# First layer of a two-layer trunk: x's projection by two plain pairs and ten of Strassen's seven products, memory gates moved into the output projection

## The chip, the cores and the metric

The kernel runs on one core of one Trainium2 chip. The metric is the device time of that core in microseconds (us). A core has five engines that run their own instruction streams and wait for each other by semaphores: TensorE (PE; its weight load PEld is listed apart), VectorE (DVE), ScalarE (ACT), GpSimd (POOL) and SyncE (SP), which here issues the DMAs between DRAM and SBUF. Products are accumulated in PSUM banks.

## The reference

Two layers act on x (1024 tokens by 1024 features), with 256 memory tokens beside it. The first layer, cut to what matters:

```python
h = x @ w_in                                    # columns: main 1024 | memory queries 512 | main gates 1024 | memory gates 512
u, q, g_main, g_mem = split(h)
y_main = pool(u)                                # group i of 256 features: mean over the last 2/4/8/16 tokens, less the token,
                                                # times pool_w[i] (256 x 256) and pool_scale
y_mem = softmax(q k^T / sqrt(128)) v            # 4 heads; k | v = mem @ w_mem_kv
y = concat(y_main * silu(g_main), y_mem * silu(g_mem))
x = layer_norm(alpha * x + y @ w_out)
```

The second layer has the same frame; its main branch is an attention with 16 heads. Everything is float32.

## The kernel before, in words

**Arithmetic.** TensorE's fast format keeps fewer bits than float32. So each operand is split: `high` is the operand rounded to that format, `low` the rest (`hi_lo`, lines 134 to 137: ScalarE copies, VectorE subtracts; `split_w`, from line 139, does it with a tile of weights that a DMA brings into the ring `raw` of three tiles). A product is then three matmuls: high x high, high x low, low x high.

**Layout.** x is held transposed, features on the 128 partitions, as eight tiles high and eight low (`A`). 128 output features by 1024 tokens are a *slab* (`slab`, L168): two accumulators of 128x512 in the PSUM ring `pj` (three banks), 8 feature tiles x 2 halves x 3 = 48 matmuls of 128x512, two weight tiles of 128 x 512. What comes out is handed to a function: copied (`u`), split (queries), or made a gate (`gate`: tanh on ScalarE, one operation on VectorE). Other PSUM rings are `L` (two banks), `T` (two, for transposes) and `O` (one).

**Order of the first layer.** 24 slabs are computed from x. `load_x` brings the eight tiles of x and splits them, while the first slabs' matmuls follow. `pool_group(0)`: two slabs of u, window sums on VectorE (1 to 4 additions of 128x1024 for each half, then `pm`, mean less token, and its split), two slabs of gates, the small product with `pool_w` (24 matmuls), times the gates, store to `y0d` in DRAM. Then `mem_kv` (keys and values of the memory), `mem_attention` (four slabs of queries; then, for eight blocks of 128 tokens, logits, softmax, transposes of the probabilities, `values`; between these steps `Fill` pumps the four slabs of memory gates so that TensorE has something to do; at its end the gates are multiplied in and the four heads stored), and `pool_group(1)` to `(3)`. GpSimd takes no part in any of this.

**Output projection** (`out_proj`, L315). 24 weight tiles of 128x512 go through `raw`, are split, and stay in tiles that later stages do not need yet. For four strips of 256 tokens the three quarters of y (`src`, in the order 2, 0, 1, where 2 is the memory's) are loaded from DRAM, split and multiplied: 144 matmuls a strip. Then comes the layer norm and the transposes that make the next layer's x.

**Who sets the order.** The program is written in this sequence; a scheduler of the language decides each engine's order from it by its own model of costs, except where `manual_schedule` fixes the written order, before for TensorE inside `mem_attention` alone. SyncE issues its DMAs in order, and an instruction that waits holds back those behind it on its engine.

Of the kernel before, what the change touches and what calls it, by code (L numbers as in the profile page):

```python
# [23 lines left out]
MH = 4  # L24
# [43 lines left out]
def trunk_kernel(ctx, tc, x, xT, memT, win, wk, wv0, wv, wmk, wmv, wout, poolw, pscale, lng, lnb, bforget, out):  # L68
# [28 lines left out]
    def ps(shape, tag, bufs):  # L97
        return psum.tile(shape, F32, tag=tag, name=nm(tag), bufs=bufs)
# [7 lines left out]
    def MK(shape, dt=F32R):  # L106
        return sb(list(shape), "MK", 4, dt)
# [10 lines left out]
    def w_slots(tags, where):  # L118

        def tiles(k):  # L120
            tag, bufs = tags[k]
            if tag == "w":
                return [[wt([P, NH]) for _ in range(2)] for _ in range(2)]
            if tag == "MK":
                pair = [MK([P, 2, NH]) for _ in range(2)]
            elif tag == "PG":
                pair = [sb([P, 2, NH], "P", 4, F32R), sb([P, 2, NH], "G", 4, F32R)]
            else:
                pair = [sb([P, 2, NH], tag, bufs, F32R, where) for _ in range(2)]
            return [[t[:, j, :] for j in range(2)] for t in pair]  # L130

        return tiles
# [55 lines left out]

    def gate(acc, dst):

        nc.scalar.activation(dst, acc, AF.Tanh, scale=0.5)
        nc.vector.scalar_tensor_tensor(dst, dst, 1.0, acc, ALU.add, ALU.mult)

    def mem_kv(l):
# [8 lines left out]
        for h in range(MH):  # L203
            acc = ps([P, NH], "pj", 3)
            for pc in range(2):
                a, b = split_w(wmk[l, h, pc], [P, 4, P])
                for k in range(4):
                    for i, (w, m) in enumerate(((a, mh), (a, ml), (b, mh))):
                        nc.tensor.matmul(
                            acc[:, :NMEM], w[:, k, :], m[pc][:, k, :],  # L210
                            start=pc == 0 and k == 0 and i == 0, stop=pc == 1 and k == 3 and i == 2,
                        )
            hi_lo(kh[:, h, :], kl[:, h, :], acc[:, :NMEM])
        accs = [ps([P, NH], "pj", 3) for _ in range(2)]
# [25 lines left out]
    def mem_attention(l, XH, XL, kv, qtile, ytile, yd):  # L240

        kh, kl, vh, vl = kv
        qs = []
        for h in range(MH):
            qh, ql = qtile(), qtile()
            run(slab(win[l, 8 + h], XH, XL, lambda cols, acc: hi_lo(qh[:, cols], ql[:, cols], acc)))
            qs.append((qh, ql))
        ys, gs = [ytile() for _ in range(MH)], [G() for _ in range(MH)]
        pt, fill = {}, Fill()
        for h in range(MH):  # L250
            fill.add(gate_units(win[l, 20 + h], gs[h], XH, XL), SLAB)

        def probs(i):
            p = sb([P, MH, NMEM], "P", 4)
            m, ms, sm, r = tiny(MH), tiny(MH), tiny(MH), tiny(MH)
            for hp in range(2):
                lg = ps([P, 2, NMEM], "L", 2)
                for j in range(2):
                    h = 2 * hp + j
                    qh, ql = (t[:, i * P : (i + 1) * P] for t in qs[h])  # L260
                    mm3(lg[:, j, :], ((qh, kh[:, h, :]), (qh, kl[:, h, :]), (ql, kh[:, h, :])))
# [3 lines left out]
                for j in range(2):  # L265
                    h = 2 * hp + j
                    nc.scalar.activation(
                        p[:, h, :], lg[:, j, :], AF.Exp, bias=ms[:, h : h + 1], scale=MSCALE, accum_out=sm[:, h : h + 1],
                    )
            nc.vector.reciprocal(r, sm)  # L270
            for h in range(MH):
                nc.vector.tensor_scalar(p[:, h, :], p[:, h, :], r[:, h : h + 1], 0.5, ALU.mult, ALU.mult)
# [11 lines left out]
        def values(c, h):  # L284
# [7 lines left out]
            nc.vector.tensor_copy(ys[h][:, c * 2 * P : (c + 1) * 2 * P], acc)  # L292
# [18 lines left out]
        for h in range(MH):  # L311
            nc.vector.tensor_tensor(ys[h], ys[h], gs[h], ALU.mult)  # L312
            nc.sync.dma_start(yd[:, h, :], ys[h])

    def out_proj(l, wtile, yd, resid, XH, XL, dst):  # L315
# [7 lines left out]
        for kk in (4, 5, 0, 1, 2, 3):  # L323
# [7 lines left out]
        for sp in range(ST // 2):  # L331
            accs = [[ps([P, NH], *bank) for _ in range(2)] for bank in (("pj", 3), ("L", 2))]
            for c in (2, 0, 1):
                src, yh, yl = T([P, 4, 2 * P], F32), T([P, 4, 2 * P]), T([P, 4, 2 * P])
                nc.sync.dma_start(src, yd[c, :, :, sp * 2 * P : (sp + 1) * 2 * P])
                hi_lo(yh, yl, src)
                for a in range(2):
                    for nh in range(2):
                        for k in range(4):
                            kt = 4 * c + k  # L340
                            wh, wl = (w[kt % 2] for w in ws[nh][kt // 2])
                            for i, (y, w) in enumerate(((yh, wh), (yh, wl), (yl, wh))):
                                nc.tensor.matmul(  # L343
                                    accs[a][nh], y[:, k, a * P : (a + 1) * P], w,
                                    start=kt == 8 and i == 0, stop=kt == 7 and i == 2,
# [31 lines left out]
    XH, XL = (sb([P, KT, S], "A", 2, F32R) for _ in range(2))  # L377

    def load_x(kt, parts=1):
        r = T(dt=F32)  # L380
        for i in range(parts):
            cols = slice(i * S // parts, (i + 1) * S // parts)
            nc.sync.dma_start(r[:, cols], xT[kt, :, cols])
            hi_lo(XH[:, kt, cols], XL[:, kt, cols], r[:, cols])

    first = [[split_w(win[0, 0, 0], [P, 4, P])], []]
    load_x(0, 2)
    first[1].append(split_w(win[0, 1, 0], [P, 4, P]))
    for kt in range(1, 4):
        load_x(kt)  # L390
    for f in range(2):
        first[f].append(split_w(win[0, f, 1], [P, 4, P]))
    for kt in range(4, KT):
        load_x(kt)
    nc.sync.dma_start(psc, pscale)
    nc.vector.tensor_scalar(pschalf, psc, 0.5, None, ALU.mult)

# [4 lines left out]
    with tc.tile_pool(name="in0", bufs=1) as in0:  # L402

        def bt():
            return sb([P, S], "B", 8, F32R, in0)

        def pool_group(g):
            w = WINDOWS[g]
            pms = []
            for f in (2 * g, 2 * g + 1):  # L410
                u = sb([P, S], "P", 4)
                run(slab(
                    first[f] if g == 0 else win[0, f], XH, XL, lambda cols, acc: nc.scalar.copy(u[:, cols], acc),
                    ("L", 2) if f == 1 else ("pj", 3),
                ))
                cur, sh = u, 1
                while sh < w:
# [3 lines left out]
                    cur, sh = nxt, 2 * sh  # L421
                pm = G()
                nc.vector.scalar_tensor_tensor(pm[:, w - 1 :], cur[:, w - 1 :], 1.0 / w, u[:, w - 1 :], ALU.mult, ALU.subtract)
                nc.vector.tensor_tensor(pm[:, : w - 1], cur[:, : w - 1], invc[:, : w - 1], ALU.mult)
                nc.vector.tensor_tensor(pm[:, : w - 1], pm[:, : w - 1], u[:, : w - 1], ALU.subtract)
                ph, pl = T(), T()
                hi_lo(ph, pl, pm)
                pms.append((ph, pl))
            r = raw([P, 2, 2 * P])
            nc.sync.dma_start(r, poolw[g])  # L430
            wh, wl = (MK([P, 2, 2 * P]) for _ in range(2))
            hi_lo(wh, wl, r)
            ys = []
            for f in (2 * g, 2 * g + 1):
                y = sb([P, S], "Y", 4, F32, in0)
                run(gate_units(win[0, 12 + f], y, XH, XL))
                ys.append(y)
            for d in range(2):
                f = 2 * g + d
                for n in range(2):  # L440
                    acc = ps([P, NH], "pj", 3)
# [10 lines left out]
        pool_group(0)  # L452
        kv = mem_kv(0)
        mem_attention(0, XH, XL, kv, bt, lambda: sb([P, S], "Y", 4, F32, in0), y0d[2])
        for g in range(1, 4):
            pool_group(g)

        XH1, XL1 = (sb([P, KT, S], "A", 2, F32R) for _ in range(2))
        wtags = [("MK", 4)] * 2 + [("W", 4)] * 2 + [("B", 8)] * 4 + [("Y", 4)] * 2 + [("PG", 0), ("w", 0)]
        out_proj(0, w_slots(wtags, in0), y0d, x, XH1, XL1, x1)  # L460
# [3 lines left out]
    with tc.tile_pool(name="in1", bufs=1) as in1:  # L464
# [8 lines left out]
        mem_attention(1, XH, XL, kv, xy, lambda: vt([P, S], F32), y1d[2])  # L473
# [320 lines left out]
```

## Time and profile before

| | us |
|---|---|
| median of three runs | 1358.33 (1356.74 to 1360.92) |
| profiled execution | 1357.83, of which the span 1356.1 |
| granted TensorE clock, mean | 0.999 of full speed |

The profiled span falls into these stages; the columns are busy times. They follow TensorE's own order, so a stage ends where the next one's matmuls begin.

| stage | from - to, us | PE | DVE | ACT | POOL |
|---|---|---|---|---|---|
| x arrives, slabs of group 0 | 0 - 50.7 | 47.9 | 28.6 | 22.8 | 0.7 |
| small product of group 0 | 50.7 - 56.2 | 5.5 | 3.5 | 1.9 | 0 |
| memory's keys and values | 56.2 - 79.6 | 23.1 | 12.8 | 10.2 | 0 |
| query slabs | 79.6 - 123.8 | 43.8 | 12.0 | 10.4 | 0 |
| memory attention with gate slabs | 123.8 - 203 | 79.1 | 53.0 | 34.9 | 0 |
| pool groups 1 to 3 | 203 - 345.7 | 142.7 | 75.3 | 38.2 | 0 |
| output projection begins | 345.7 - 400 | 50.5 | 33.4 | 19.3 | 0 |
| its rest, second layer | 400 - 1356 | 939.3 | 529.3 | 388.8 | 275.7 |

How to read it: an engine's busy time in a stage, set against the stage's length, says how much room it has there. A slab's 48 matmuls make 10.9 us, so the 24 slabs are 262 us, some 19% of the span. The page counts 131.48 MB moved by DMA, a mean of 97 GB/s; DMA engines are at most half busy in any of 40 equal slices.

### The profile page before, as it was taken

The page shows a single profiled execution, that of the slowest core. Times are in us where ns is not written, and L with a number is a line of the kernel's source. Part 1 is how long each engine was busy: PE and PEld are TensorE (multiplying, and loading weights), DVE is VectorE, ACT ScalarE, POOL GpSimd, SP SyncE. Part 2 cuts the span into 40 slices and gives each one's busy share as a digit, 9 for nine tenths or more (in the row PEclk, how much of TensorE's full clock was granted, in tenths as well). Part 3 has the DMA queues.
Part 4 walks back from the last instruction along what each step waited for, and adds up shares of the span by engine and source line. Part 5 has one row for each costly group of instructions (what it writes and reads, how often), then busy time and mean ns, then how long its engine had stood idle before and what let it go on. Part 6 is the DMA issues. An engine that isn't in the chain of part 4 may idle for free. (4 is left out here: it accounts for less than half of the span.)

```text
span 1356.1 us, 19185 instructions
## 1 busy us (share of the span) xinstructions
PE 1332.0 (98%) x6962; PEld 1124.2 (83%) x6962; DVE 747.8 (55%) x1594; ACT 526.4 (39%) x1124; POOL 276.4 (20%) x388
## 2 busy tenths in 40 slices
PE   9999999999999999999999999999999999999997
PEld 6878888888778888888988888888888888878886
DVE  6433675446555573467445564556554655665543
ACT  5333432223321132344235554555455555553110
POOL 0000000000000000000054545464545455521000
PEclk9999999999999999999999999999999999999999
DMA  5331112223653242103230213122312222355331
GB/s 210 130 112 47 32 58 83 78 83 112 203 185 109 94 136 89 48 21 111 67 119 24 87 55 110 47 91 59 105 44 94 71 86 75 128 195 191 135 109 47
DMA packets 65614, 131.48 MB, mean 97 GB/s; under 512 B 7280, under 2 KB 20848, under 8 KB 65520
## 3 DMA queue, kind: packets, MB, share of 16 engines
q1 hardware_dynamic: 65520, 130.26, 28.8%
q8 instruction: 55, 0.90, 0.3%
q14 instruction: 39, 0.32, 0.1%
HBM read 99.17 MB, written 22.68 MB: 90 GB/s over the span
## 5 line engine op out<-in xcount | busy, mean ns | idle before, releaser
L178 PE MATMUL pj<-A,w 128*128 128x512 f32 x2928 | 754.5, 398 | 1.9 <-ACT A L136 1.4
L178 PEld LDWEIGHTS pj<-A,w 128*128 128x128 f32 x2928 | 525.5, 189 | 95.6 <-ACT A L136 2.6
L137 DVE TENSOR_TENSOR T<-T,T 128x512 fp32r<-128x512 f32 (+2 forms) x248 | 151.8, 637 | 164.2 <-ACT T L136 108.0
L136 ACT CAST T<-T 128x512 fp32r<-128x512 f32 (+2 forms) x248 | 128.9, 548 | 161.9 <-PE T L233 62.6
L622 ACT ACTIVATE P<-P,s 128x128 f32<-128x128 f32 (+7 forms) x128 | 99.5, 777 | 141.6 <-DVE s L620 140.8
L613 POOL TENSOR_SCALAR P<-R,cumn 128x128 f32<-128x128 f32 (+7 forms) x128 | 96.3, 753 | 215.9 <-PE T L233 148.7
L147 DVE TENSOR_TENSOR w<-raw,w 128x512 fp32r<-128x512 f32 x102 | 69.9, 689 | 115.5 <-ACT w L146 115.1
L524 POOL MEMSET G<- 128x128 f32 x1 | 0.2, 204 | 634.5 <-DVE V L312 634.5
L146 ACT CAST w<-raw 128x512 fp32r<-128x512 f32 x102 | 63.3, 622 | 159.3 <-PE pj L178 108.6
L233 PE MATMUL T<-ident,P 128*128 128x128 f32 x704 | 101.4, 272 | 2.0 <-DVE V L137 1.1
L233 PEld LDWEIGHTS T<-ident,P 128*128 128x128 f32 x704 | 84.9, 140 | 20.4 <-issue 1.7
L655 PEld LDWEIGHTS O<-T,V 128*128 128x128 f32 x640 | 85.0, 190 | 11.9 <-DVE T L137 5.9
L166 PE MATMUL L<-B,B 128*128 128x512 f32 (+3 forms) x384 | 88.9, 339 | 1.1 <-DVE s L620 1.1
L655 PE MATMUL O<-T,V 128*128 128x256 f32 (+1 forms) x640 | 85.6, 278 | 3.3 <-DVE T L137 3.1
L166 PEld LDWEIGHTS L<-B,B 128*128 128x128 f32 x384 | 71.6, 188 | 17.1 <-DVE s L620 1.7
L620 DVE CUSTOM_DVE_ANT_0 P<-L,P 128x512 f32<-128x512 f32 (+3 forms) x128 | 72.7, 568 | 14.4 <-PE L L166 10.5
L147 POOL TENSOR_TENSOR w<-raw,w 128x512 fp32r<-128x512 f32 x54 | 70.0, 1296 | 4.5 <-PE pj L178 0.9
L661 DVE TENSOR_TENSOR G<-O,G 64x256 f32<-64x256 f32 x64 | 27.0, 422 | 72.1 <-ACT G L660 71.3
L343 PE MATMUL pj<-B,T 128*128 128x512 f32 x216 | 52.2, 390 | 0.5 <-DVE B L137 0.5
L343 PE MATMUL L<-B,T 128*128 128x512 f32 x216 | 51.9, 389 | 0.0
L343 PEld LDWEIGHTS pj<-B,T 128*128 128x128 f32 x216 | 40.5, 188 | 9.3 <-DVE B L137 0.9
L343 PEld LDWEIGHTS L<-B,T 128*128 128x128 f32 x216 | 40.5, 188 | 8.4
(175 smaller groups left out, 1541.2 us busy)
## 6 DMA issues: line engine op xcount, KB each, us to landing
raw<-in_win_dram SPq DMA_DIRECT2D x96, 256.0 KB, 2.5
raw<-in_wout_dram SPq DMA_DIRECT2D x48, 256.0 KB, 3.0
B<-B SPq DMA_DIRECT2D x64, 128.0 KB, 2.3
R<-cumd SPq DMA_DIRECT2D x16, 512.0 KB, 3.5
y0d<-Y SPq DMA_DIRECT2D x12, 512.0 KB, 2.9
T<-y0d SPq DMA_DIRECT2D x12, 512.0 KB, 4.0
T<-y1d SPq DMA_DIRECT2D x12, 512.0 KB, 4.6
raw<-in_wmk_dram SPq DMA_DIRECT2D x16, 256.0 KB, 2.6
```

Source lines behind the costliest of these rows:

```text
L136: nc.scalar.copy(hi, src)
L137: nc.vector.tensor_tensor(lo, src, hi.bitcast(F32), ALU.subtract)
L146: nc.scalar.copy(h, r)
L147: (nc.gpsimd if low[0] else nc.vector).tensor_tensor(l, r, h.bitcast(F32), ALU.subtract)
L166: nc.tensor.matmul(acc, a, b, start=i == 0, stop=i == len(terms) - 1)
L178: nc.tensor.matmul(accs[n], a[:, k, :], b[:, kt, n * NH : (n + 1) * NH], start=kt == 0 and i == 0, stop=kt == KT - 1 and i == 2,)
L233: nc.tensor.transpose(t[:, j, :], src[:, (4 * g + j) * P : (4 * g + j + 1) * P], ident)
L343: nc.tensor.matmul(accs[a][nh], y[:, k, a * P : (a + 1) * P], w, start=kt == 8 and i == 0, stop=kt == 7 and i == 2,)
L613: nc.gpsimd.tensor_scalar(p[:, :L], R[:, :L], 1.0, cumn[:, i * HEADS + hd : i * HEADS + hd + 1], ALU.mult, ALU.add)
L620: nc.vector.tensor_tensor_reduce(p[:, lo:up], lg, p[:, lo:up], 1.0, top, ALU.add, ALU.min, m[:, n : n + 1])
L622: nc.scalar.activation(p[:, :L], p[:, :L], AF.Exp, bias=top, scale=-1.0, accum_out=sums[:, 8 * (hd % 2) + i : 8 * (hd % 2) + i + 1])
L655: nc.tensor.matmul(acc[:, w:], st, t[j // 4][:, j % 4, w:], start=j == 0 and e == 0, stop=j == last and e == 1,)
```

## The change

**Projection of x.** The 24 slabs become 12 pairs of two. Two pairs (the queries) are computed plainly (`plain_pair`): 96 matmuls in four accumulators. The other ten go through `winograd`: the pair's weights form a matrix of 2 x 2 blocks (two slabs by two halves of the features), x one of 2 x 2 blocks (two halves of the features by two halves of the tokens), and Winograd's form of Strassen's product needs seven block products of 12 matmuls in place of eight, 84 in all. For it `sums_of_x` forms T1 to T4 once (16 subtractions of 128x512 on GpSimd, and the splits of the results), and each pair forms four sums of its weights on GpSimd, while the products' results are added up on VectorE (seven evacuations: one copy on ScalarE, six additions).

**Queries** are stored split to DRAM (`qd`) and each block of 128 tokens loads its own. **Memory gates** are no longer multiplied in the attention: they are stored to DRAM (`gd`), and `out_proj` loads them and multiplies them into the memory's quarter of y. Its quarters come in the order 2, 1, 0. **Softmax's normalisation** moves from VectorE to ScalarE. **Pooling** (`pooled`) becomes a generator whose steps (`chore`) are issued between the products of the following pair; the groups run 3, 2, 1, 0, with the next group's u (`pool_in(g - 1)`) ahead of this group's small product (`pool_out(g)`), which takes its accumulators from `L`. **Order**: TensorE's order is written out by hand (`manual_schedule`) from the start to the last `pool_out`. Tiles: the ring `B` of eight goes, `A2` (six, T2 to T4), `raw2` (four), `Y` (two) and other places for output weights come.

The diff's core (unchanged statements and the second layer's same steps, now written at the call, are left out):

```diff
+    def chore(n):
+        while n and chores:
+            if next(chores[0], chores) is chores:
+                chores.pop(0)
+            else:
+                n -= 1
+    def winograd(w, X, banks, temps, out):
+        f32, spare = temps
...
+        def add(dst, a, b):
+            nc.vector.tensor_tensor(dst, a, b, ALU.add)
+        def less(dst, a, b):
+            nc.gpsimd.tensor_tensor(dst, a, b, ALU.subtract)
+            return dst
+        left, right = slice(0, NH), slice(NH, S)
+        u = spare()
+        u2, u3 = u[:, 0, :], u[:, 1, :]
+        a11, a12 = load(0, 0, f32()), load(0, 1, f32())
+        a21, a22 = load(1, 0, raw([P, 4, P])), load(1, 1, raw([P, 4, P]))
+        s1, s2 = f32(), f32()
+        def sums():
+            nc.gpsimd.tensor_tensor(s1, a21, a22, ALU.add)
+            return less(s2, s1, a11)
+        def fifth(acc):
+            add(u2, acc, u2)
+            out(1, right, acc, u3)
+        steps = (
+            ("B11", lambda: a11, lambda acc: nc.scalar.copy(u2, acc)),
+            ("B21", lambda: a12, lambda acc: out(0, left, acc, u2)),
+            ("T2", sums, lambda acc: add(u2, acc, u2)),
+            ("T3", lambda: less(a21, a11, a21), lambda acc: add(u3, acc, u2)),
+            ("T1", lambda: s1, fifth),
+            ("T4", lambda: a22, lambda acc: out(1, left, acc, u3)),
+            ("B22", lambda: less(s2, a12, s2), lambda acc: out(0, right, acc, u2)),
+        )
+        ahead = split(steps[0][1]())
+        for j, (name, _, took) in enumerate(steps):
+            (h, l), (xh, xl) = ahead, X[name]
+            if j < 6:
+                ahead = split(steps[j + 1][1]())
+            acc = ps([P, NH], *banks)
+            for k in range(4):
+                for i, (a, b) in enumerate(((h, xh), (h, xl), (l, xh))):
+                    nc.tensor.matmul(acc, a[:, k, :], b[:, k, :], start=k == 0 and i == 0, stop=k == 3 and i == 2)
+                    since[0] += NH
+                    if k == 3 and i == 2:
+                        took(acc)
+                        chore(2)
+                    yield NH
@@ probs, in mem_attention
+            nc.vector.tensor_scalar(sm, sm, 2.0, None, ALU.mult)
             nc.vector.reciprocal(r, sm)
             for h in range(MH):
-                nc.vector.tensor_scalar(p[:, h, :], p[:, h, :], r[:, h : h + 1], 0.5, ALU.mult, ALU.mult)
+                nc.scalar.activation(p[:, h, :], p[:, h, :], AF.Copy, scale=r[:, h : h + 1])
-        for h in range(MH):
-            nc.vector.tensor_tensor(ys[h], ys[h], gs[h], ALU.mult)
-            nc.sync.dma_start(yd[:, h, :], ys[h])
@@ out_proj
+        order = (2, 0, 1) if gates is None else (2, 1, 0)
-            for c in (2, 0, 1):
+            for c in order:
                 src, yh, yl = T([P, 4, 2 * P], F32), T([P, 4, 2 * P]), T([P, 4, 2 * P])
                 nc.sync.dma_start(src, yd[c, :, :, sp * 2 * P : (sp + 1) * 2 * P])
+                if c == 2 and gates is not None:
+                    gt = sb([P, 4, 2 * P], "P", 4)
+                    nc.sync.dma_start(gt, gates[:, :, sp * 2 * P : (sp + 1) * 2 * P])
+                    nc.vector.tensor_tensor(src, src, gt, ALU.mult)
                 hi_lo(yh, yl, src)
@@ the first layer
+        def load_x(kt):
+            t = sb([P, 2, NH], "P", 4) if kt < 4 else G((P, 2, NH))
+            nc.sync.dma_start(t.rearrange("p a b -> p (a b)"), xT[kt])
+            for n in range(2):
+                h, l = X[place[kt // 4][n]]
+                hi_lo(h[:, kt % 4, :], l[:, kt % 4, :], t[:, n, :])
+            quarters.append(t)
+        place = (("B11", "T4"), ("B21", "B22"))
+        def sums_of_x():
+            t12s = []
+            for k in range(4):
+                (b11, b12), (b21, b22) = ((t[:, 0, :], t[:, 1, :]) for t in (quarters[k], quarters[4 + k]))
+                t12s.append(T((P, 2, NH), F32))
+                t1, t2 = (t12s[k][:, j, :] for j in range(2))
+                nc.gpsimd.tensor_tensor(t1, b12, b11, ALU.subtract)
+                nc.gpsimd.tensor_tensor(t2, b22, t1, ALU.subtract)
+                for n, t in (("T2", t2), ("T1", t1)):
+                    hi_lo(X[n][0][:, k, :], X[n][1][:, k, :], t)
...
+                nc.gpsimd.tensor_tensor(t3, b22, b12, ALU.subtract)
+                nc.gpsimd.tensor_tensor(t4, b21, t12s[k][:, 1, :], ALU.subtract)
+                for n, t in (("T3", t3), ("T4", t4)):
+                    hi_lo(X[n][0][:, k, :], X[n][1][:, k, :], t)
+        def plain_pair(h0, loads):
+            accs = [[ps([P, NH], *b) for b in banks] for banks in ((("pj", 3), ("pj", 3)), (("pj", 3), ("L", 2)))]
...
+                if kt == KT - 1:
+                    for n in range(2):
+                        t = sb([P, 2, NH], "Y", 2, F32R, in0)
+                        hi_lo(t[:, 0, :], t[:, 1, :], accs[d][n])
+                        nc.sync.dma_start(qd[:, :, h0 + d, n * NH : (n + 1) * NH], t.bitcast(F32))
+        def gates_to(dst):
+            def out(d, cols, acc, add):
+                y = dst(d, cols)
+                t = G((P, NH))
+                nc.vector.tensor_tensor(y, acc, add, ALU.add)
+                nc.scalar.activation(t, y, AF.Tanh, scale=0.5)
+                nc.vector.scalar_tensor_tensor(y, t, 1.0, y, ALU.add, ALU.mult)
+            return out
+        def queries(i):
+            for j in (i, i + 1):
+                if j < ST and j not in ahead:
+                    ahead[j] = G((P, 2, MH, P), F32R)
+                    nc.sync.dma_start(ahead[j].bitcast(F32), qd[:, :, :, j * P : (j + 1) * P])
...
+        def pool_in(g):
+            us = [sb([P, S], "P", 4) for _ in range(2)]
+            def out(d, cols, acc, add):
+                nc.vector.tensor_tensor(us[d][:, cols], acc, add, ALU.add)
+            run(pair(2 * g, out))
+            pms = []
+            chores.append(pooled(g, us, pms))
+            return pms
+        def pool_gates(g):
+            ys = [sb([P, S], "Y", 2, F32, in0) for _ in range(2)]
+            run(pair(12 + 2 * g, gates_to(lambda d, cols: ys[d][:, cols])))
+            return ys
+        def pool_out(g, pms, ys):
+            while len(pms) < 2:
+                chore(1)
             r = raw([P, 2, 2 * P])
             nc.sync.dma_start(r, poolw[g])
-            wh, wl = (MK([P, 2, 2 * P]) for _ in range(2))
+            wh, wl = (wt([P, 2, 2 * P]) for _ in range(2))
...
+        with tc.manual_schedule(engines={PE}):
+            plain_pair(0, True)
+            plain_pair(2, False)
+            sums_of_x()
+            nc.sync.dma_start(psc, pscale)
+            nc.vector.tensor_scalar(pschalf, psc, 0.5, None, ALU.mult)
+            kv = mem_kv(0, lambda: queries(0))
+            for h0 in (0, 2):
+                fill.add(gates_out(h0), PAIR)
+            mem_attention(kv, queries, fill, took)
+            following = pool_in(3)
+            for g in (3, 2, 1, 0):
+                ys, pms = pool_gates(g), following
+                if g:
+                    following = pool_in(g - 1)
+                pool_out(g, pms, ys)
...
+        out_proj(0, w_slots(wtags, in0), y0d, x, XH1, XL1, x1, gd)
```

## The prediction, made before the changed kernel ran

> **What bounds the kernel now.** I read the page first (busy time by engine, the 40 slices), then TensorE's timeline through the first layer, then VectorE and GpSimd by form, then SyncE's timeline at the places where the change moves loads.
>
> ```profile
> span 1356.1 us, 19185 instructions
> PE 1332.0 (98%) x6962; PEld 1124.2 (83%) x6962; DVE 747.8 (55%) x1594; ACT 526.4 (39%) x1124; POOL 276.4 (20%) x388
> POOL 0000000000000000000054545464545455521000
> 28.97 21.92 PE L178 MATMUL pj<-A,w 128*128 128x512 f32 x96
> 247.74 43.68 PE L178 MATMUL pj<-A,w 128*128 128x512 f32 x192
> 291.26 5.60 PE L166 MATMUL pj<-T,MK 128*128 128x512 f32 x24
> 345.66 0.62 PE L343 MATMUL pj<-MK,T 128*128 128x512 f32 x2
> 384.00 1.52 PE L343 MATMUL pj<-MK,T 128*128 128x512 f32 x6
> ```
>
> TensorE is busy 98% of the span and waits for next to nobody: the kernel lasts as long as its matmuls. In the first layer 192 matmuls of a group (start 247.74 to the start of the next row, 291.26) take 43.52 us, 0.2267 us each, without a gap. VectorE has nearly half of its time free, GpSimd does nothing in the first layer (zeros up to slice 20). So a matmul taken away is time gained, as long as the others keep up with what replaces it.
>
> **1. Matmuls removed: -27.2 us.** Before, 24 slabs of 48 matmuls; after, two plain pairs of 96 and ten pairs of 84. The built program shows the same: 120 fewer 128x512 matmuls and no other change in TensorE's work. 120 x 0.2267 = 27.2. The second layer's order on TensorE is unchanged but for one matmul's place, so all else happens before 400 us.
>
> What is added lies on VectorE and GpSimd. Their prices:
>
> ```profile
> L147 DVE TENSOR_TENSOR w<-raw,w 128x512 fp32r<-128x512 f32 x21 | 14.5, 690 | 35.4 <-ACT w L146 35.4
> L137 DVE TENSOR_TENSOR T<-G,T 128x1024 fp32r<-128x1024 f32 x6 | 7.4, 1226 | 6.0 <-ACT T L136 6.0
> L147 POOL TENSOR_TENSOR w<-raw,w 128x512 fp32r<-128x512 f32 x54 | 70.0, 1296 | 4.5 <-PE pj L178 0.9
> 1175.31 1.28 POOL L147 TENSOR_TENSOR w<-raw,w 128x512 fp32r<-128x512 f32 x1
> 1175.43 0.68 DVE L192 SCALAR_TENSOR_TENSOR G<-G,pj 128x512 f32<-128x512 f32 x1
> 1176.56 2.39 POOL L670 TENSOR_TENSOR R<-R,G 128x1024 f32<-128x1024 f32 x1
> 1177.06 2.44 DVE L137 TENSOR_TENSOR MK<-raw,MK 128x512 fp32r<-128x512 f32 x1 [0.62 <-ACT MK L136]
> ```
>
> A 128x512 VectorE operation takes 0.69 us, in a row 0.61 (341.21, 341.82, 342.42 us are three starts); a 128x1024 one 1.22, in a row 1.14; tiny ones about 0.15. A GpSimd 128x512 operation takes 1.30. The last four rows matter most. VectorE's operation that reads PSUM and SBUF runs beside GpSimd at its usual 0.68. The one that reads two SBUF tiles, started at 1177.06 while GpSimd works until 1178.95, takes 2.44 in place of 0.69: it waits until GpSimd is done. All "low = source - high" operations of weights and x read two SBUF tiles, and the change puts 16 GpSimd operations beside them at the start and 4 into each of ten pairs.
>
> **2. The start: +17 us (bounds 1 and 18).** The first plain pair runs while x arrives, as before (the first half tile of x becomes a whole one, about +1). But `sums_of_x` now stands among it: in VectorE's order the splits of T1, T2 and T3 come before the low part of the first query tile, and the second plain pair needs that query's accumulator (`pj` has three buffers, all in use). So ahead of the second pair VectorE must do 16 splits of x, 12 of T, five of weights and the query's, 34 x 0.62 = 21.1 us; GpSimd does 16 x 1.296 = 20.7; they exclude each other, and the first x is there at about 4.5 us (before, the first matmul on x starts at 4.85): 4.5 + 21.1 + 20.7 = 46. Before, the 97th matmul starts at 28.97. 46 - 29 = 17. If the two engines ran side by side, only the +1 would be left.
>
> **3. Memory attention: +5 us (3 to 8).** The queries go through DRAM (8 stores and 8 loads of 512 KB; DMA share in these stages is 0.1 to 0.3, two iterations of lead): nothing. Normalising moves to ScalarE (44% busy there), VectorE's additions replace it: nothing. But the block is now closed by hand: the last transposes and four `values` have no slab of the following group among them, as before they had (195 to 203 us). Transposes to high and low parts: 0.59 + 0.69 and hops, about 1.8; the one `O` bank is emptied three times, 0.42 and hops, 0.75 each; softmax's last steps perhaps 0.7. Together 4.8.
>
> **4. The pool groups: +20 us (4 to 26).** A pair lasts 84 x 0.2267 = 19.0 us. In `pool_gates(3)` VectorE's list, from the last evacuation of the pair before to the first weight split of the next, has 17 operations of 512, 11 of 1024 (window sums, `pm`, its low part) and 11 tiny: 10.4 + 12.5 + 1.7 = 24.6, and 1.3 of waiting for the second product. The split of the next pair's first weights stands behind all of it, so TensorE waits 24.6 + 1.3 - 19.0 = 6.9, less 0.45 since the low part is needed at the third matmul: 6.4. In `pool_gates(2)` (7 of 1024) the sixth product's low part comes at 15.4 us of the pair where 14.05 would do, the seventh's 0.4 late, and the next pair's first split stands behind the last evacuation, 2.0: 3.8. In `pool_gates(1)` likewise 1.4 + 1.0: 2.4. Three `pool_out` wait 0.5 each for an `L` bank. Sum 14. GpSimd's four operations (5.2 us) fall into each of these lists; of each list a third reads PSUM or is waiting, and runs on. I take 2 per gates pair, 6 in all; nothing, or 4 each, are the ends. Before, none of these waits exists.
>
> **5. The output projection: +20 us (15 to 24).**
>
> ```profile
> 64.08 1.87 SPq L141 DMA_DIRECT2D raw<-in_wmv_dram  x3
> 68.11 0.33 SPq L141 DMA_DIRECT2D raw<-in_wmv_dram  x1
> 74.82 0.33 SPq L141 DMA_DIRECT2D raw<-in_win_dram  x1
> 326.43 0.62 SPq L335 DMA_DIRECT2D T<-y0d  x1
> 345.17 0.53 SPq L335 DMA_DIRECT2D T<-y0d  x1
> DMA to landing us min/median/max: 3.7/3.9/7.7
> ```
>
> The memory gates come from DRAM now, and are multiplied in before the first matmul of the projection. In SyncE's order this load stands behind 23 of the 24 weight loads, and SyncE issues in order; before, the first `T<-y0d` went out at 326.43, after five weight tiles. Weight loads go through three `raw` tiles; such a tile comes round in 4.0 us (64.08, 68.11: load, cast, low part), or eight loads in 74.82 - 64.08 = 10.74, 1.34 each. Let t0 be the end of the last `pool_out` on TensorE. The tile that held the pool weights is free at t0 - 8.2 (its split stands behind the evacuation of the fifth gates product, which ends 48 matmuls, 10.9 us, ahead of t0). Twenty loads later, t0 - 8.2 + 20 x 1.34 = t0 + 18.6, the gates' load goes out; it lands 3.9 later (a 128x4x256 tile, as `T<-y0d`), then 1.22 for the product, 1.05 for the cast, hops: t0 + 26. Nothing stands in TensorE's order to fill this. All weights are there by then, so nothing is lost afterwards. Before, the first two rows took 384.00 - 345.66 = 38.3 for 144 x 0.2267 = 32.6: 5.7 lost. 26 - 5.7 = 20.
>
> **Sum**: -27.2 + 17 + 5 + 20 + 20 = +34.8. The profiled execution took 1357.83 (span 1356.1, 1.7 around it), 0.5 below the median 1358.33: 1357.8 + 34.8 = 1393.
>
> **Rivals.**
> A. *GpSimd and VectorE do not exclude each other at the start and in the pairs.* Then 2 is 1 and 4 is 14: +12.8, 1371. For it: only a few such rows, all in another stage. Against: all of them agree. 10%.
> B. *TensorE slows after long waits.* The change makes about four gaps of 4 us and more; before, none after the start passes 1.7. The nine 128x512 warm-up matmuls of the kernel's first microseconds take 3.49 us, 0.39 each against 0.227, which hints at a slow start after idling. Nine such matmuls after each gap: 4 x 1.5 = 6, so 1399. The granted clock is 9 or more in every slice of before, so it can't show. 20%. The Trainium skill ("TensorE: Matmul & The Clock Gate", Part 1: The HAM clock gate) says that the array falls to half its clock after an idle window of about 3.4 us and needs as much busy time to come back; by that each gap would cost up to 1.7 to 3.4 us, an estimate from that page, and the sum would be 1400 to 1406. No run here shows it yet.
> C. *The weights' stream starts earlier* (SyncE's long lists filled while VectorE idles, or a shorter turn of `raw`): 5 shrinks to 10, 1383. 10%.
> D. *Faster: VectorE keeps ahead.* Its place is the gates pair, its price is terms 2 and 4 and half of 5. If GpSimd ran beside it and its lists fitted in the 19.0 us, then -27.2 + 1 + 4 + 0 + 10 = -12, 1346. It decides from where a list of 24.6 becomes 19.0. Against: the 24.6 are counted from rows, without any exclusion. 5%.
> That the matmuls are not saved is excluded by the built program.
>
> **Chances**: forecast 55%, A 10, B 20, C 10, D 5. Around no change (within 0.3%, 4 us, about what a measurement of this kernel can tell): only if A and C hold together, 4% taken out of these two. Range: 1368 takes in A, 1405 takes in B and the upper end of 4; outside are D, A with C, and a start or a weight stream worse than counted.
>
> **What would show it.** The second plain pair starts near 46 us (step 2); gaps of 4 to 6 us behind each of `pool_gates(3)`, `(2)` (step 4); VectorE's two-SBUF operations lasting over 1 us where GpSimd works (A falls); no output-projection matmul for some 20 us while `raw<-in_wout` streams (step 5); granted clock below 9 in a slice (B). I am wrong if TensorE's busy share in the first layer stays at 98%.

## The result, and the profile after

The changed kernel took 1406.53 us (1401.09 to 1408.38), before 1359.49: a ratio of 1.0342, 95% interval 1.0307 to 1.0376. Forecast were 1393 and a range of 1368 to 1405, which it lies just above: the direction was right, and the loss of 35 us was too small: it is 47. The profiled execution was the shortest of its four, 1401.09 (span 1399.3), 43.3 above the one of before. The account below explains those 43.

The page of the changed kernel:

```profile
span 1399.3 us, 19362 instructions
PE 1323.0 (95%) x6842; PEld 1111.2 (79%) x6842; DVE 833.2 (60%) x1669; ACT 575.7 (41%) x1235; POOL 364.2 (26%) x444
PE   7999999889479999999999999999999999999997
POOL 6020121222000000000015465455445454622000
PEclk9999999999889999999999999999999999999999
```

TensorE has 120 instructions less, but its busy share falls from 98 to 95%: slices 1, 8, 9, 11 and 12 show where. GpSimd now works in the first layer, most in slice 1. PEclk, the granted clock, falls below 9 in two slices; before it did in none.

The same kernel by stages (start:end in us, length, busy time of each engine with instructions, granted clock, DMA share):

```profile
0.00:42.70 42.70, 32.62 (x105) 22.06 (x106) 38.03 (x59) 21.36 (x38) 26.89 (x22) 0.92 0.47 161
166.66:367.00 200.34, 184.27 (x770) 148.37 (x768) 153.45 (x225) 61.29 (x97) 44.43 (x28) 0.96 0.26 78
367.00:392.07 25.07, 0.01 (x1) 0.00 (x0) 13.10 (x20) 10.82 (x17) 0.00 (x0) 0.60 0.79 251
535.77:1399.30 863.53, 845.66 (x4647) 723.31 (x4646) 470.06 (x1084) 382.79 (x865) 277.10 (x382) 1.00 0.30 90
```

The first row is the time until the second plain pair, in which VectorE is busy for 38 of 42.7 us; the second holds the pool groups; the third is a hole of 25 us in which TensorE does nothing; the last is the second layer, which is as before. The same instruction of the second layer's `mem_kv` stands at 495.25 us before and 538.17 after, 42.9 later, so everything happens ahead of it.

| term | predicted | found in the traces |
|---|---|---|
| 1 matmuls removed | -27.2 | -27.2 (120 x 0.2267) |
| 2 start | +17 | +15.3: second pair at 42.70 against 28.97; then 0.7 in it and 0.9 in `mem_kv` |
| 3 memory attention | +5 | +7.0: 77.2 less 168 x 0.2267 for the gate pairs leaves 39.1; before, 79.6 to 345.66 less 1032 x 0.2267 (20 slabs, three small products) leaves 32.1 |
| 4 pool groups | +20 | +26.3: 200.3 less 768 matmuls of 0.2267 |
| 5 output projection | +20 | +21.6: from the last `pool_out` to the second layer 171.2 against 149.6 |
| sum | +34.8 | +43.0 (measured 43.3) |

TensorE's timeline in the pool groups and behind them (start, duration, what, in brackets the idle time before and what ended it):

```profile
206.01 5.49 PE L259 MATMUL pj<-A,w 128*128 128x512 f32 x12 [3.35 <-DVE w L142]
213.79 20.51 PE L259 MATMUL pj<-A,w 128*128 128x512 f32 x82 [2.29 <-DVE w L142]
257.99 7.35 PE L259 MATMUL pj<-A,w 128*128 128x512 f32 x24 [3.45 <-DVE w L142]
266.88 18.90 PE L259 MATMUL pj<-A,w 128*128 128x512 f32 x82 [1.53 <-DVE w L142]
309.48 25.94 PE L259 MATMUL pj<-A,w 128*128 128x512 f32 x106 [3.45 <-DVE w L142]
392.07 3.33 PE L419 MATMUL pj<-MK,T 128*128 128x512 f32 x6 [25.06 <-ACT T L141]
```

Read waits and durations apart. The waits of `pool_gates(3)`, `(2)` and `(1)` and those of `pool_out` sum to 16.1. Then see what follows a wait: 12 matmuls take 5.49, 0.46 each in place of 0.23; 82 take 20.51 behind a wait of 2.29, but 18.90 behind one of 1.53. TensorE runs at half speed for a while after the longer waits. These slow stretches hold 2.6 + 1.8 + 1.8 + 1.8 = 8 us in the groups and 1.8 at the output projection. The 2 us of the 26.3 that are left lie in small pieces.

The stall at 392.07 on SyncE:

```profile
369.69 15.43 SPq L400 DMA_DIRECT2D raw<-in_wout_dram  x12
385.17 0.58 SPq L410 DMA_DIRECT2D P<-gd  x1
```

The load of the gates goes out at 385.17, behind 12 weight loads that each wait for a `raw` tile; 385.6 was predicted.

The start on GpSimd and VectorE:

```profile
14.38 1.74 POOL L491 TENSOR_TENSOR T<-G,P 128x512 f32<-128x512 f32 x1
16.07 1.73 POOL L492 TENSOR_TENSOR T<-G,T 128x512 f32<-128x512 f32 x1
16.59 1.76 DVE L142 TENSOR_TENSOR A<-T,A 128x512 fp32r<-128x512 f32 x1
21.65 1.77 DVE L152 TENSOR_TENSOR w<-raw,w 128x512 fp32r<-128x512 f32 x1
42.70 0.96 PE L510 MATMUL pj<-A,w 128*128 128x512 f32 x3 [0.99 <-DVE Y L142]
```

Both engines fall into one beat: VectorE's operation takes 1.76 in place of 0.69, GpSimd's 1.73 in place of 1.30; in 1.7 us there is one of each.

### The profile page after: what moved, and what is told of

It is laid out like the page before. It is cut to its first block, busy times and chain, and to the rows that moved or that the text cites. A ratio compares the mean times of both kernels' runs of the same rounds, so it can differ in the third digit from the quotient of the medians.

```text
span 1399.3 us, 19362 instructions
## 1 busy us (share of the span) xinstructions
PE 1323.0 (95%) x6842; PEld 1111.2 (79%) x6842; DVE 833.2 (60%) x1669; ACT 575.7 (41%) x1235; POOL 364.2 (26%) x444
## 3 DMA queue, kind: packets, MB, share of 16 engines
HBM read 105.46 MB, written 28.97 MB: 96 GB/s over the span
## 4 chain that ended last, share of the span: by engine, by line
PE 74%; DVE 12%; DMA 4%; ACT 4%; issue 3%; POOL 1%; DVEq 0%; ACTq 0%; SPq 0%; POOLq 0%
PE pj L183 26%; PE pj L259 10%; PE pj L419 9%; PE L L419 9%; PE L L171 5%; PE T L314 5%; PE O L864 4%; DMA raw<-in_wout_dram 2%; PE pj L704 2%; PE O L171 2%; DMA raw<-in_wmv_dram 1%; DVE P L829 1%; DVE A L142 1%; DVE T L142 1%; DVE G L584 1%
## 5 line engine op out<-in xcount | busy, mean ns | idle before, releaser
L183 PE MATMUL pj<-A,w 128*128 128x512 f32 x1824 | 494.2, 402 | 0.6 <-DVE MK L142 0.6
L183 PEld LDWEIGHTS pj<-A,w 128*128 128x128 f32 x1824 | 320.5, 189 | 51.4 <-DVE MK L142 1.1
L259 PE MATMUL pj<-A,w 128*128 128x512 f32 x840 | 204.9, 402 | 14.1 <-DVE w L142 14.1
L259 PEld LDWEIGHTS pj<-A,w 128*128 128x128 f32 x840 | 160.7, 194 | 49.3 <-DVE w L142 16.5
L141 ACT CAST w<-raw 128x512 fp32r<-128x512 f32 x78 | 48.0, 620 | 107.8 <-PE pj L259 84.6
L224 POOL TENSOR_TENSOR raw<-raw,raw 128x512 f32<-128x512 f32 x30 | 45.4, 1519 | 129.1 <-DVE w L142 87.3
L152 DVE TENSOR_TENSOR w<-raw,w 128x512 fp32r<-128x512 f32 x62 | 45.7, 740 | 46.9 <-ACT w L151 46.4
L142 DVE TENSOR_TENSOR w<-raw,w 128x512 fp32r<-128x512 f32 x78 | 57.5, 742 | 10.8 <-ACT w L141 10.7
```

Of the source, the lines that this page charges most:

```text
L141: nc.scalar.copy(hi, src)
L142: nc.vector.tensor_tensor(lo, src, hi.bitcast(F32), ALU.subtract)
L152: (nc.gpsimd if low[0] else nc.vector).tensor_tensor(l, r, h.bitcast(F32), ALU.subtract)
L183: nc.tensor.matmul(accs[n], a[:, k, :], b[:, kt, n * NH : (n + 1) * NH], start=kt == 0 and i == 0, stop=kt == KT - 1 and i == 2,)
L259: nc.tensor.matmul(acc, a[:, k, :], b[:, k, :], start=k == 0 and i == 0, stop=k == 3 and i == 2)
```

## The experiments

Each runs beside the kernel before; ratios are to it. All but the sixth are edits of the changed kernel.

**1. The gates ahead of the weights.** In `out_proj`, with the other strips as they were; `memory_quarter` holds the removed lines, loads, product and split:

```diff
+        early = memory_quarter(0) if gates is not None else None
         gb = []
...
+                if c == 2 and gates is not None:
+                    yh, yl = early if sp == 0 else memory_quarter(sp)
```

> The changed kernel, with the memory's quarter of y for the first strip (its loads, the product with the gates and the split) issued ahead of the 24 output-weight loads. In the changed kernel TensorE stands still for 25.1 us (367.0 to 392.07) ahead of the output projection. Theory (step 5: the gates' load is queued behind the weights on SyncE): the first matmul of the projection comes 2 to 6 us after the last pool_out, not more than 6 us are lost between the strips, and the kernel is 18 to 22 us shorter than the changed kernel's 1401 to 1408. Rival 1 (the weights' stream itself is what is late: all 24 tiles take 25 us, and the early matmuls only wait later for their own weights): the gap is cut into smaller ones with nearly the same sum, and the gain is below 8 us. Rival 2 (C of the prediction): between these, 10 us.

1381.13 us, ratio 1.0162 (1.0144 to 1.0180), 25 us less than the changed kernel, more than the 18 to 22 expected (the profiled executions differ by 19.8). TensorE's timeline:

```profile
362.75 4.28 PE L171 MATMUL L<-T,w 128*128 128x512 f32 x18
366.86 0.85 PE L428 MATMUL pj<-MK,T 128*128 128x512 f32 x3
382.22 2.85 PE L428 MATMUL pj<-A,T 128*128 128x512 f32 x11 [0.81 <-ACT A L141]
```

The projection's first matmuls now stand among those of the last `pool_out`, and the longest later wait up to 402 us is 1.39. The hole was the place of one load in SyncE's order. The weights' stream was not what TensorE stood still for.

**2. The sums of x on VectorE.**

```diff
-                nc.gpsimd.tensor_tensor(t1, b12, b11, ALU.subtract)
+                nc.vector.tensor_tensor(t1, b12, b11, ALU.subtract)
...
```

> The changed kernel, with the 16 sums of x (T1 to T4) on VectorE in place of GpSimd. In the changed kernel the second plain pair starts at 42.70 us; VectorE's and GpSimd's operations there last 1.7 us each in alternation. Theory (step 2: the two exclude each other): VectorE's list gets 16 operations longer, but each takes 0.62, and the second plain pair starts at 28 to 36 us; the kernel is 7 to 16 us shorter (the upper end with TensorE back at full clock at the start). Rival (x's arrival or VectorE's own work limits the start): the second pair starts at 42.7 or, with 16 x 0.62 = 9.9 us more on VectorE, up to 10 us later; no gain or a loss.

1390.41 us, ratio 1.0234 (1.0217 to 1.0251), 16 less, the upper end of what was expected. VectorE and TensorE:

```profile
22.70 1.29 DVE L483 TENSOR_TENSOR T<-P 128x512 f32<-128x512 f32 x2
25.71 1.89 DVE L142 TENSOR_TENSOR A<-T,A 128x512 fp32r<-128x512 f32 x3
28.66 5.66 PE L510 MATMUL pj<-A,w 128*128 128x512 f32 x23
```

VectorE does more and is done sooner. Ahead of the first query's low part (at 27.52 here, at 41.97 in the changed kernel) it has 37 operations in place of 33, and they take 0.6 each in place of 1.1; no matmul waits between 10 us and the second pair, which starts at 28.66 (28.97 before the change). GpSimd's own pace was not the limit: fifteen operations of 1.30 from 8.03 on would have ended at 27.5 (an estimate), and the last one ended at 37.8. So the 13.7 of the first pair came from two engines that exclude each other; neither VectorE's own work nor the arrival of x shows as a wait. One thing differs besides: the scheduler put fewer sums ahead of the query. In the changed kernel's order four more sums and four more splits would stand there, some 4.8 us at 0.6 each (an estimate), so up to that much of the 14 us is owed to the order. The Trainium skill (SBUF — State Buffer, "Who interferes with whom") says that a VectorE instruction with two SBUF inputs contends with a GpSimd instruction that reads SBUF, as an exclusive lock. By that rule the trace agrees, 1.76 against 0.69.

**3. One step of the pooling per product.**

```diff
-                        chore(2)
+                        chore(1)
```

> The changed kernel, with one step of the pooling instead of two issued after each of the products, so that the pooling of a group is spread over the gates pair and the following pair. In the changed kernel TensorE waits 3.35 + 2.29 us in pool_gates(3) and behind it, 3.45 + 1.53 in (2), 3.45 in (1), and runs at a lower clock behind these waits. Theory (step 4: VectorE's list is longer than the pair's 19.0 us): a list of 24.6 falls to about 19, most of the 14 us of waiting goes, and with it the low clock; 10 to 20 us shorter. Rival (GpSimd's exclusion of VectorE in the pairs makes the waits, whatever the pooling): the waits stay within 2 us of what they were, gain below 5 us.

1386.14 us, ratio 1.0203 (1.0187 to 1.0218), 20 less, again the upper end. The pool groups' longest waits:

```profile
211.95 3.03 PE L259 MATMUL pj<-A,w 128*128 128x512 f32 x12 [0.61 <-DVE w L142]
216.65 10.72 PE L259 MATMUL pj<-A,w 128*128 128x512 f32 x46 [1.67 <-DVE w L142]
231.37 3.06 PE L171 MATMUL L<-T,w 128*128 128x512 f32 x12 [1.28 <-DVE Y L632]
```

Waits of 3.35, 2.29 and 3.45 are gone, and with them every slow stretch there: 12 matmuls take 3.03. The same work, spread over two pairs instead of one, fits but for some 6 us of short waits.

**4. The sums of the weights on VectorE** (`less` and `sums` with `nc.vector`).

> The changed kernel, with the four sums of a pair's weights on VectorE in place of GpSimd. VectorE's list of each pair gets 4 x 0.61 = 2.4 us longer and loses what GpSimd's four operations cost it. Step 4 of the prediction took 2 us per gates pair for that exclusion, between 0 and 4: at 2 the kernel stays within 2 us of the changed kernel (ratio to before about 1.033); at 0 each of the three gates pairs waits 2.4 longer, some 7 us slower and more with the lower clock; at 4 it is 4 to 6 us faster.

1394.30 us, ratio 1.0269 (1.0252 to 1.0286), 12 less by the medians, beyond the upper end, and 6.5 by the profiled executions. In the changed kernel, `pool_gates(2)`:

```profile
247.43 2.17 POOL L235 TENSOR_TENSOR raw<-raw,raw 128x512 f32<-128x512 f32 x1 [4.18 <-DVE w L142]
248.37 1.78 DVE L537 SCALAR_TENSOR_TENSOR Y<-G,Y 128x512 f32<-128x512 f32 x1
250.07 1.25 DVE L585 COPY G<-G 128x4 f32<-128x4 f32 x1
262.59 1.28 DVE L590 TENSOR_TENSOR G<-G,invc 128x7 f32<-128x7 f32 x1
```

Even operations of 0.15 us wait for GpSimd and take 1.25. With the sums on VectorE the same place of TensorE's timeline is this:

```profile
255.57 6.02 PE L259 MATMUL pj<-A,w 128*128 128x512 f32 x24 [1.26 <-DVE w L142]
```

Two of the delays (1.78 for 0.69, 1.25 for 0.15) stand ahead of the wait of 3.45; they make 2.2, and the wait is 2.2 shorter now. The third (1.28 for 0.15) stands ahead of the next wait. So the exclusion cost 3.3 in this pair, where 2 was taken. VectorE's additional sums cost nothing there: of them only one falls into this stretch, and VectorE waits for TensorE both before and after it. All pool groups together are 6.6 us shorter (193.7 against 200.3), slow stretches included, where the prediction took 6 for the exclusion. And a wait of 1.26 is not followed by a full slow stretch: 24 matmuls take 6.02 in place of 7.35.

**5. Matmuls in the waits.** Extra matmuls ahead of the third of a product, in the gaps shown above:

```diff
+                    if k == 0 and i == 1 and j in keep:
+                        busy = ps([P, NH], "O", 1)
+                        for _ in range(keep[j]):
+                            nc.tensor.matmul(busy, a[:, 0, :], b[:, 0, :], start=True, stop=True)
```

> The changed kernel, with extra 128x512 matmuls (12, 8, 12, 5 and 12; results unused, in the otherwise idle O bank) placed where TensorE waits in the five gaps of the pool groups. They fit into the waits, so they cost nothing if the waits stay. Theory (rival B: TensorE is slower for a while after a long wait): the 12 matmuls after the first gap take 2.9 in place of 5.49 us, the stretches after the other gaps lose their extra 1.7 us each, the granted clock stays at 1.0 from 200 to 340 us; since part of it turns into a longer wait for VectorE, 3 to 8 us shorter. Rival (the slow matmuls come from something else, such as the operands' arrival or contention): the stretches after the gaps keep their length and the kernel gains nothing, or loses up to 49 x 0.23 = 11 us.

1399.67 us, ratio 1.0306 (1.0291 to 1.0321): 5 less than the repeat of the changed kernel (experiment 6), 7 less than its first runs. The timeline, where O rows are the extra ones:

```profile
202.61 2.88 PE L259 MATMUL O<-A,w 128*128 128x512 f32 x12
206.11 3.02 PE L255 MATMUL pj<-A,w 128*128 128x512 f32 x12 [0.62 <-DVE w L142]
213.91 21.66 PE L255 MATMUL pj<-A,w 128*128 128x512 f32 x82 [2.96 <-DVE w L142]
309.04 3.01 PE L255 MATMUL pj<-A,w 128*128 128x512 f32 x12 [0.73 <-DVE w L142]
312.66 21.61 PE L255 MATMUL pj<-A,w 128*128 128x512 f32 x94 [0.60 <-DVE w L142]
```

The data come at the same time (206.11 against 206.01), and 12 matmuls take 3.02 in place of 5.49. This gap alone would not show why: the repeat has 3.02 there with nothing added. The gap in `pool_gates(1)` does. The five traces with an idle 3.45 there all lose 1.6 to 1.8 us behind it (25.94 for 106 matmuls in the changed kernel); with 12 extra matmuls in the wait the same 106 take 3.01 and 21.61, 0.3 too long. Rival B's mechanism is shown: idling makes TensorE slow. But at the first gap the 2.5 us gained turn into a longer wait for VectorE at the second gap, where the eight extra ones do not reach: 2.96, and 82 matmuls then take 2.9 too long. A slow stretch that ends in a wait for another engine costs nothing; only the last ahead of a free run does. The granted clock from 200 to 340 us is 0.98, where 1.0 was expected (0.94 in the changed kernel). The pool groups are 1.3 us shorter in this execution and the wait ahead of the projection 1.4 longer; where the medians' 5 to 7 us come from, the trace does not show.

**6. The changed kernel again.**

> The changed kernel again, unchanged: its profiled execution was the shortest of its four (1401.1, the others 1405.6 to 1408.4). Theory (rival B: which of the waits are followed by a slow stretch differs from execution to execution): an execution of 1404 to 1408 shows the same waits within 1 us and slow stretches after more of them, or longer ones. Rival (something else differs, such as a later load): the difference is in the length of a wait or in another part of the span.

1404.87 us, ratio 1.0345 (1.0330 to 1.0360); the profiled span is 1402.4, 3.1 longer than the first.

```profile
206.03 3.02 PE L259 MATMUL pj<-A,w 128*128 128x512 f32 x12 [3.35 <-DVE w L142]
213.82 20.83 PE L259 MATMUL pj<-A,w 128*128 128x512 f32 x82 [4.78 <-DVE w L142]
393.62 3.33 PE L419 MATMUL pj<-MK,T 128*128 128x512 f32 x6 [26.25 <-ACT T L141]
```

The first wait of 3.35 is followed by no slow stretch here, but the next wait is 2.5 longer, and by the next group the two executions are 0.4 apart. The wait ahead of the projection is 1.2 longer (it is 25.0 to 26.9 in the six other traces with this order of loads), the projection then takes 0.8 longer, most of it slow matmuls, and the second layer 0.8. So the theory of this run falls in the main: the clock does differ from execution to execution, but it makes less than 1 of the 3.1 us. Why three of the first four executions take some 4 to 7 us more than the profiled one stays open.

**7. Two banks at the end of memory attention** (O and L in turn for the last four `values`).

> The changed kernel, with the last four products of probabilities and values in two alternating PSUM banks (O and L) in place of O alone. Step 3 of the prediction priced the emptying of that one bank at 0.75 three times. Theory: the waits of 0.68, 0.61 and 0.52 us behind these products go, 1.5 to 2 us of TensorE's timeline at 162 to 166 us; in the whole time that is at the edge of what can be measured. Rival (the values wait for the transposed probabilities or VectorE's queue, not for the bank): under 0.5 us.

1403.06 us, ratio 1.0330 (1.0314 to 1.0345). The stage goes from 77.23 to 75.14 us (91.33 to 166.47), and the waits of 0.68, 0.61 and 0.52 are gone. The mechanism of step 3 is shown for the bank's part; in the whole time the change is inside the spread.

**8. Experiments 1, 2 and 3 together.**

> The three edits together: the first strip's memory quarter ahead of the weight loads, the sums of x on VectorE, one step of pooling per product. Alone they gave 25, 16 and 20 us. Theory (three separate losses, at three places of the first layer): they add up, 1406.5 - 61 = 1345, 1342 to 1352, 1% faster than before: the 27.2 us of matmuls less the rest of the waits. Rival (the losses hide one another: with the start early, some other engine or the weights' stream sets the pace): 1358 or more, no gain against before.

1346.33 us, ratio 0.9916 (0.9901 to 0.9930): 0.8% less than before, and the whole interval lies below 1. The three losses stood one behind the other and add up, 61 us expected and 60 measured.

**9. The same with the sums of the weights on VectorE.**

> As the three edits together, and the sums of the weights on VectorE too, so that GpSimd does nothing in the first layer. With one step of pooling per product VectorE's list is about 19 us in a gates pair; 2.4 more would make it the bound again if GpSimd's exclusion costs less than that: 0 to 8 us slower than the three edits together. If GpSimd's four operations cost VectorE over 2.4 us per pair, it is 0 to 5 us faster.

1344.64 us, ratio 0.9916 (0.9890 to 0.9942): no difference that can be told. Three runs took 1344 to 1345, the profiled one 1351.70; the slow products of the last section are in its trace, and its second layer is 3.7 us longer than in experiment 8. That the exclusion is hidden once the lists fit in a pair is the likely reading; it was not tested apart.

**10. And the two banks.**

> The three edits together, the sums of the weights on VectorE, and the two alternating banks at the end of memory attention. The version with the sums on VectorE had three runs of four at 1344.4 to 1344.9 and one at 1351.7, whose trace shows slow products at the end of memory attention (1.6 us in place of 0.95 each, three of them). Theory: without the short waits there, TensorE stays at full clock and 1.5 us of waiting goes: 1342 to 1344 and no run above 1347. Rival: no difference, 1344 to 1352.

1343.34 us (1342.06 to 1345.10), ratio 0.9893 (0.9876 to 0.9910), the lowest median, though within 2 us of experiment 9. Its page:

```profile
span 1341.8 us, 19308 instructions
PE   9999999999999999999999999999999999999997
PEclk9999999999999999999999999999999999999999
```

TensorE is at 98% as before, with 120 matmuls less.

**11. The new order without Strassen.** In experiment 1's kernel, all pairs plain, no sums, and results taken as they are:

```diff
-            sums_of_x()
...
+                for kt in range(KT):
+                    h, l = halves[kt // 4]
+                    xh, xl = X[(("B11", "T4"), ("B21", "B22"))[kt // 4][n]]
```

> The whole of the new order, with the first strip's memory quarter ahead of the weight loads, but all twelve pairs computed plainly: 96 matmuls a pair, no sums of x or of weights, each result taken from its accumulator as it is. This undoes step 1 alone. Theory (the 27.2 us of step 1 are real and the new order by itself gains nothing): 120 matmuls more than the three edits together (1346), so 1373 less the few us of waiting that its pairs still have, 1364 to 1374: slower than before by 0.4 to 1.2%. Rival (the gain of the three edits against before comes from the new order and not from fewer matmuls): 1358 or less.

1358.49 us, ratio 1.0010 (0.9998 to 1.0022): the time of before. So the rest of the change (queries and gates through DRAM, hand-written order, the groups' new sequence), with the load moved as in experiment 1, costs nothing by itself, and the gain of experiment 8 comes from fewer matmuls. But 1364 to 1374 was expected, and that missed. Up to the second layer this kernel and that of experiment 8 differ by 13.6 us, not 27.2 (498.14 against 484.54 for the same instruction). With Strassen, 3.2 are lost again in memory attention, 6.0 in the pool groups and 4.3 in the output projection; the first would be some 1.7 larger but for the slow products that this execution had (last section), and what makes the third was not tested. Even in the mended kernel, half of the saving is spent.

## Why the prediction was wrong, step by step

- **Step 1** held: 27.2 us of matmuls are gone, and experiments 8 and 11 together show that they are worth something.
- **Step 2** held, with its mechanism: 42.70 against the predicted 46 for the second pair, 28.66 when GpSimd is left out (and fewer sums stand ahead). The two engines' times do not quite add (1.7 for a pair of operations, where 0.62 + 1.30 was used).
- **Step 3** held in part. It was 7 in place of 5, within its bounds. The close of the block, to which the prediction put all of it, loses about 4 (157.20 to 166.66 us; its matmuls make 5.4 by their spacing before the change), of which the bank's share is 2. Another 3.1 us of waits lie in the block's middle, from 113 to 137 us, which the prediction had at nothing.
- **Step 5** held to 2 us: 25.06 of standing still against 26, the load at 385.17 against 385.6.
- **Step 4 is the one that failed**: 26.3 in place of 20. Not by the waits: 16.1 us of them were found (18.6 in the repeat, experiment 6), and the prediction had 20, 14 from the counted lists and 6 for the exclusion. The 6 were about right as a whole, though `pool_gates(2)` alone had 3.3 in place of 2 (experiment 4). What failed is that step 4 priced the matmuls behind the waits at 0.2267 each, their slowness at nothing. "TensorE slows after long waits" was put down as a rival, at 1.5 us a gap and 20%, where it belongs into the sum: it is in every trace with waits over 2.2 us, 1.6 to 2.9 us behind nearly each. In this stage that is 8 us, though some 2.5 of them are absorbed by the wait that follows (5.6 in the repeat, where the first gap has none), and 1.8 more stand at the output projection, which step 5 did not count either.
- **Rivals.** A falls with experiment 2. C falls with the load's time. D names the right condition, lists that fit into the pair; experiment 3 makes it nearly true. That experiment 8 then took the 1346 that D gave is luck: D had 4 us for memory attention, none for the pool groups and 10 for the projection, and its trace, set against before, has 7.3, 8.8 and -0.6 us there. B is right in its mechanism and in its direction: with it in the sum, at its own price of 6, the forecast would have been 1399.
- **What stays open**: the median is 1405 to 1407 and the profiled executions were 1401 and 1404. The account covers the profile; some 2 to 5 us of the median are not explained.

The Trainium skill (TensorE: Matmul & The Clock Gate, Part 1: The HAM clock gate) gives half clock after an idle window of about 3.4 us. Half clock agrees (0.46 against 0.23 us a matmul). The length does not: waits of 2.29 (the changed kernel), 2.50 (experiment 1) and 2.96 us (experiment 5) were followed by slow stretches too, and a wait of 3.35 once was not (experiment 6).

## What to carry to other kernels

Removing work from the engine that is the bound pays only as far as the others keep up in each stage: compare the list of the engine that replaces it with the length of the stage, piece by piece, before counting the gain. Look up where a new load stands in its queue and which two engines' operands exclude each other; together they cost 37 us here, with 27 saved, and both went when instructions were moved. Price each new wait of 2.3 us and more on TensorE at the wait and a slow stretch of about 1.7 us behind it, unless another wait follows at once.

## What the runs showed of the hardware

- TensorE's half-speed stretch after a wait is seen, in the pool groups and at the output projection, behind all but two of the waits of 2.29 us and more (3.35 in experiment 6, where nothing is lost, and 3.45 in experiment 1, where 0.4 is); it loses 1.6 to 2.9 us. Behind waits of up to 1.67 us at most 0.4 is lost there, but for what comes next.
- Many short waits do it as well. At the end of memory attention of the kernel without Strassen, six narrow matmuls take 1.65 in place of 0.98 us:

```profile
149.29 1.38 PE L171 MATMUL O<-T,MK 128*128 128x256 f32 x6 [0.52 <-DVE Y L551]
151.28 1.62 PE L171 MATMUL O<-T,MK 128*128 128x256 f32 x6 [0.61 <-DVE Y L551]
153.41 1.65 PE L171 MATMUL O<-T,MK 128*128 128x256 f32 x6 [0.52 <-DVE Y L551]
```

The same waits in the changed kernel left them at 0.94 to 0.98. Of the ten traces with these waits four have slow products (experiments 2, 4, 9 and 11), and the matmuls behind lose up to 2.2 us more (158 take 38.24 in experiment 2, 36.00 in the changed kernel). Which of the two happens was not settled.
- While GpSimd works, VectorE's operations with two SBUF inputs, and even a copy of 128x4, take up to 1.1 us longer in these rows, whatever their size: 0.15 becomes 1.25, 0.69 becomes 1.78.
